# Dense products of an MLP and two gated stages by seven quarter products in place of eight

## Chip, cores and metric

One core of one Trainium2 chip runs the program. The metric is the device time of one execution in microseconds, the median of several executions.

## What is computed

Two transformer-like blocks on 1024 tokens of width 1024, float32, one after the other. Cut to what matters here:

```python
def first_block(x, ...):
    ...                                   # mixer: pooling, gated linear recurrence, w_out
    z = rms_norm(h, norm_mlp_g)
    h = h + square(relu(z @ w_up)) @ w_down          # 1024 -> 4096 -> 1024
    z = rms_norm(h, norm_ple_g)
    h = h + sigmoid(z @ w_ple_gate + b_ple_gate) * (p @ w_ple_proj)
    return rms_norm(h, norm_final_g)

def swiglu(x, w_in, w_out):
    gate, up = split(x @ w_in, 2)                    # 1024 -> 2 x 2816
    return (silu(gate) * up) @ w_out                 # 2816 -> 1024

def second_block(x, ...):
    x = x + 0.5 * rms_norm(swiglu(rms_norm(x, ffn1_pre_g), ffn1_w_in, ffn1_w_out), ffn1_post_g)
    ...                                   # mixer: dilated attention and an S5 state space model
    return x + 0.5 * rms_norm(swiglu(rms_norm(x, ffn2_pre_g), ffn2_w_in, ffn2_w_out), ffn2_post_g)
```

## The kernel before

Every dense product is made exact enough by splitting both factors into a rounded part (`wh`, `zh`, `hh`; made on ScalarE with a copy) and a remainder (`wl`, `zl`, `hl`; a subtraction) and adding three products in one PSUM bank: high x high, high x low, low x high. So each 128x128 by 128x512 block of a product is three matmuls.

Weights come in pieces of 128 x 1024. `raw` loads a piece through SP's queue into one of two buffers, `fetch` rounds it on ScalarE (L282) and takes the remainder on GpSimd (L283), and `plan`, `prefetch` and `take` keep up to `NW` = 5 pieces ready ahead of their use.

A stage begins when the stage before has finished the 1024 tokens as 8 tiles of 128. `follow` runs a chain for each tile (residual or `seam`, root mean square, scaling into `xs`), and `Z.ready(half)` turns four scaled tiles with 32 TensorE transposes (L149) and splits the result (L166, L167). `ups_first` multiplies half 0 by the first four weight pieces before it asks for half 1. After that `ups` makes two pieces' products with all 1024 tokens, an activation follows (`relu2`, L610 to L613; `swiglu`, L804 to L807, where `hl` is the remainder on VectorE), and `down` multiplies two finished factor pieces by two weight pieces, tile by tile, and adds the sum into `X` or `Y` in SBUF on VectorE (L405). Up and down alternate in a loop, so the factor stays in SBUF for a short time only. The last four factor pieces are multiplied tile by tile with the next stage's chain behind each tile; at the very end the last tile is done in halves.

Beside the MLP lies preparation for the S5 model: `s5_small` (a chain of small VectorE operations) in step 1 of the loop and one `s5_eighth` in each of the steps 3 to 10. A scheduler puts each engine's instructions into a fixed order from the program's order and its own estimate of times; `after` gives it an order and makes no wait on the chip.

SBUF buffers have tags: 24 of 4 KB a partition under `u`, 8 under `x`, 4 under `s`; two each under `raw` and `xr`; five each under `wh` and `wl`. PSUM has eight banks of 128 x 512.

## Time and profile before

| | us |
|---|---|
| median of 3 runs | 3132.41 (3132.29 to 3135.37) |
| the profiled execution, its own time | 3131.91 |
| span of that execution, first to last instruction | 3130.1 |
| busy: TensorE, VectorE, GpSimd, ScalarE | 3024.4, 1432.0, 1030.5, 899.4 |
| mean granted TensorE clock | 0.983 |
| moved by DMA | 222.94 MB |

The stages on the time axis: first mixer to about 272 us, MLP to 980, gate of the first block to 1125, first gated stage to 1840, second mixer to 2405, second gated stage to the end. A busy share says how long an engine had an instruction in hand; matmuls overlap, so the distance between their starts is read beside it.

### The profile page before, as it was taken

How to read it: one execution, taken by the hardware profiler on the slowest of the kernel's cores; microseconds unless marked ns; L12 is line 12 of the kernel's file. 1: busy time of each engine (PE TensorE's matmuls, PEld its weight loads, DVE VectorE, ACT ScalarE, POOL GpSimd, SP SyncE). 2: the span in 40 equal slices, each digit the busy share in tenths (PEclk: the TensorE clock that was granted, in tenths of full speed). 3: DMA queues.
4: the chain of work that ended last, by engine and by line, in shares of the span. 5: the costliest groups of instructions: out<-in, count | busy, mean ns of one | idle time of the engine just before them, and what ended most of it. 6: DMA issues, size and time to landing. Idle time of an engine off the chain costs nothing. (4 is left out here: it accounts for less than half of the span.)

```text
span 3130.1 us, 34489 instructions
## 1 busy us (share of the span) xinstructions
PE 3024.4 (97%) x13761; PEld 2508.9 (80%) x13761; DVE 1432.0 (46%) x2421; ACT 899.4 (29%) x1461; POOL 1030.5 (33%) x658
## 2 busy tenths in 40 slices
...
GB/s 139 61 41 75 86 78 102 90 80 107 48 48 61 68 95 54 47 48 41 54 53 49 48 128 97 160 94 74 35 54 141 54 54 48 49 53 41 54 48 95
DMA packets 71154, 222.94 MB, mean 71 GB/s; under 512 B 15988, under 2 KB 16080, under 8 KB 70992
## 3 DMA queue, kind: packets, MB, share of 16 engines
...
## 5 line engine op out<-in xcount | busy, mean ns | idle before, releaser
L283 POOL TENSOR_TENSOR wl<-raw,wh 128x1024 fp32r<-128x1024 f32 (+1 forms) x254 | 615.2, 2429 | 1751.5 <-ACT wh L282 1737.9
L383 PE MATMUL b<-z,wh 128*128 128x512 f32 x3712 | 997.5, 390 | 0.0
L383 PEld LDWEIGHTS b<-z,wh 128*128 128x128 f32 x3712 | 695.9, 188 | 147.6 <-issue 1.7
L282 ACT ACTIVATE wh<-raw 128x1024 fp32r<-128x1024 f32 (+1 forms) x254 | 267.6, 1054 | 1555.1 <-PE b L397 526.8
L383 PE MATMUL b<-z,wl 128*128 128x512 f32 x1856 | 573.4, 389 | 0.0
L805 DVE TENSOR_TENSOR sw<-sw,b 128x512 f32<-128x512 f32 x88 | 57.0, 685 | 827.6 <-PE b L383 788.5
L383 PEld LDWEIGHTS b<-z,wl 128*128 128x128 f32 x1856 | 348.5, 188 | 72.8
L397 PE MATMUL b<-wl,hh 128*128 128x512 f32 x1216 | 375.6, 389 | 0.0
L397 PE MATMUL b<-wh,hl 128*128 128x512 f32 x1216 | 375.4, 389 | 0.0
L397 PE MATMUL b<-wh,hh 128*128 128x512 f32 x1216 | 375.2, 389 | 0.0
L405 DVE TENSOR_TENSOR Y<-b,Y 128x512 f32<-128x512 f32 x320 | 204.4, 683 | 186.3 <-PE b L397 186.3
L397 PEld LDWEIGHTS b<-wh,hh 128*128 128x128 f32 x1216 | 228.2, 188 | 47.5
L397 PEld LDWEIGHTS b<-wh,hl 128*128 128x128 f32 x1216 | 228.2, 188 | 47.4
L397 PEld LDWEIGHTS b<-wl,hh 128*128 128x128 f32 x1216 | 228.2, 188 | 47.4
L405 DVE TENSOR_TENSOR X<-b,X 128x512 f32<-128x512 f32 x272 | 174.0, 683 | 118.5 <-PE b L397 118.2
L611 DVE TENSOR_TENSOR r<-r 128x512 f32<-128x512 f32 x64 | 87.6, 1393 | 116.3 <-ACT r L610 116.3
L807 DVE TENSOR_TENSOR hl<-sw,hh 128x512 fp32r<-128x512 f32 x88 | 133.2, 1548 | 9.2 <-ACT hh L806 5.2
L1235 POOL TENSOR_SCALAR P<-P,den 128x640 f32<-128x640 f32 (+5 forms) x64 | 109.2, 1729 | 13.6 <-DVE den L1234 6.9
L368 PE MATMUL b<-z,wh 128*128 128x512 f32 x256 | 99.6, 399 | 1.3 <-DVE z L167 1.3
L369 PE MATMUL b<-z,wh 128*128 128x512 f32 x256 | 99.1, 394 | 1.2 <-DVE z L167 1.2
L370 PE MATMUL b<-z,wl 128*128 128x512 f32 x256 | 99.0, 392 | 0.0
L758 POOL TENSOR_TENSOR Y<-Y,g 128x1024 f32<-128x1024 f32 x23 | 55.5, 2414 | 104.8 <-ACT junk L302 104.8
(320 smaller groups left out, 3721.2 us busy)
## 6 DMA issues: line engine op xcount, KB each, us to landing
raw<-in_f_in SPq DMA_DIRECT2D x88, 512.0 KB, 3.5
raw<-in_f_out SPq DMA_DIRECT2D x44, 512.0 KB, 3.5
raw<-in_w_up SPq DMA_DIRECT2D x32, 512.0 KB, 3.5
raw<-in_w_down SPq DMA_DIRECT2D x32, 512.0 KB, 3.8
s5l<-s SPq DMA_DIRECT2D x24, 512.0 KB, 4.9
raw<-in_w_in SPq DMA_DIRECT2D x12, 512.0 KB, 3.5
X<-in_x SPq DMA_DIRECT2D x8, 512.0 KB, 7.5
xr<-in_x SPq DMA_DIRECT2D x8, 512.0 KB, 3.5
```

The costliest lines, as they stand in the source:

```text
L282: nc.scalar.activation(h, r, AF.Copy)
L283: nc.gpsimd.tensor_tensor(l, r, h.bitcast(F32), op=ALU.subtract)
L368: nc.tensor.matmul(pp, wh[:, k, :], z(0, k, sl), start=k == 0, stop=False)
L369: nc.tensor.matmul(pp, wh[:, k, :], z(1, k, sl), start=False, stop=False)
L370: nc.tensor.matmul(pp, wl[:, k, :], z(0, k, sl), start=False, stop=k == 7)
L383: nc.tensor.matmul(pp[n], w[:, k, :], z(m, k, slice(n * H, n * H + H)), start=k == 0 and w is wh and m == 0, stop=k == nk - 1 and w is wl)
L397: yield nc.tensor.matmul(pp, h[:, ts], w[:, sl], start=f == 0 and w is wh and h is hh, stop=f == len(hs) - 1 and h is hl)
L405: nc.vector.tensor_tensor(X[t][:, sl], pp, X[t][:, sl], op=ALU.add)
L611: nc.vector.tensor_tensor(r, r, r, op=ALU.mult)
L805: nc.vector.tensor_tensor(s, s, pu, op=ALU.mult)
L807: nc.vector.tensor_tensor(hl[:, sl], s, hh.bitcast(F32)[:, sl], op=ALU.subtract)
L1235: nc.gpsimd.tensor_scalar(out=p[:, :w], in0=p[:, :w], scalar1=den[:, c : c + 1], scalar2=None, op0=ALU.mult)
```

## The change

The three places `w_up`/`w_down`, `ffn1` and `ffn2` use a form of Strassen's scheme on quarters. For the product up, two weight pieces (256 hidden units) are one factor and the normalized input is the other; each is cut into four quarters, and seven quarter products (numbered 1 to 7) of sums and differences replace eight. `lefts` makes the weight side of a pair (rounding on ScalarE, remainders of the pieces themselves on GpSimd, sums and remainders of sums on VectorE). `ZS` makes the input side once for a stage: seven operands, each rounded and with its remainder, 28 buffers that stay in SBUF. `ups_s` runs the products so that the partial sums are added in PSUM: products 1, 6, 7 and 4 go through one bank, with a copy to SBUF after 1, 6 and 7; 5 and 3 through another; 2 has its own. The order in a round is 2, 3 of the pair before, 1, 4 of the pair before, 6, 5, 7.

For the product down all up products of the stage come first. `lay_by` makes the sums and differences of the activated factor (VectorE and GpSimd) and writes seven quarters of 128 x 512 for each 256 hidden units to DRAM. `down_s` then runs the products one after the other (2, 1, 5, 3, 6, 7, 4) over all hidden units, with four banks each: for a unit of two chunks (512 hidden units) it reads the quarter back, reads the weight quarter, subtracts where the product asks for it, and rounds both on ScalarE with both remainders on VectorE, into `wh` and `wl` buffers, two of five each. The last two units of a product are multiplied tile by tile. Tiles 0 to 3 are finished in product 6 and tiles 4 to 7 in product 4.

The S5 preparation moves between the down products (`aside`): `s5_small` ahead of product 2, five eighths in the MLP and three in the first gated stage. The tags become 32 `u` and no `x`; the two `raw` buffers are also loaded in a fixed order; the first stage's input goes to DRAM (`xm`) and is read back for the residual; the last tile is no longer done in halves.

```diff
+class ZS(Z):
+    late = "u"
+    RIGHT = {1: "B11", 2: "B21", 3: "B22", 4: "T4", 5: "T1", 6: "T2", 7: "T3"}
...
+    def __call__(self, p, k):
+        hi, lo = self.op[self.RIGHT[p]][k // 2]
+        return hi[:, k % 2], lo[:, k % 2]
...
+    def split(self, name, f, eng=None):
+        m = self.m
+        hi, lo = m.u("zh", F32R, [P, 2, H]), m.u("zl", F32R, [P, 2, H])
+        m.nc.scalar.activation(hi, f, AF.Copy)
+        (eng or m.nc.vector).tensor_tensor(lo, f, hi.bitcast(F32), op=ALU.subtract)
+        self.op.setdefault(name, []).append((hi, lo))
...
+        if half == 0:
+            for name, k0 in (("B21", 4), ("B11", 0)):
+                self.f[name] = []
+                for q in range(2):
+                    f = self.turned(0, k0 + 2 * q)
+                    self.split(name, f)
+                    self.f[name].append(f)
...
+        self.settle()
...
+        for q in range(2):
+            f12.append(self.turned(1, 2 * q))
+            v.tensor_tensor(f11[q], f12[q], f11[q], op=ALU.subtract)
+            self.split("T1", f11[q])
+        for q in range(2):
+            f22.append(self.turned(1, 4 + 2 * q))
+            v.tensor_tensor(f11[q], f22[q], f11[q], op=ALU.subtract)
+            self.split("T2", f11[q])
+        for q in range(2):
+            v.tensor_tensor(f12[q], f22[q], f12[q], op=ALU.subtract)
+            self.split("T3", f12[q])
+        for q in range(2):
+            self.split("B22", f22[q], g)
+        for q in range(2):
+            v.tensor_tensor(f21[q], f21[q], f11[q], op=ALU.subtract)
+            self.split("T4", f21[q])
...
-        self.pu = pool("u", 24)
+        self.pu = pool("u", 32)
...
+        if tag == "raw":
+            if self.last_raw:
+                self.after(d, self.last_raw)
+            self.last_raw = d
...
+        q.append(None)
...
+    def lefts(self, src1, src2):
+        nc = self.nc
+        v, g = nc.vector, nc.gpsimd
+        r1, r2 = self.raw(src1), self.raw(src2)
+        w = lambda tag: self.pw.tile([P, 2, H], F32R, name=tag, tag=tag)
+        res = {}
...
+        def split(x, first, second, eng):
+            hi, lo = w("wh"), w("wl")
+            nc.scalar.activation(hi.rearrange("p a b -> p (a b)"), x, AF.Copy)
+            eng.tensor_tensor(lo.rearrange("p a b -> p (a b)"), x, hi.bitcast(F32).rearrange("p a b -> p (a b)"),
+                              op=ALU.subtract)
+            for n, p in enumerate((first, second)):
+                res[p] = tuple(x[:, n].rearrange("p (k f) -> p k f", k=4) for x in (hi, lo))
+        split(r1, 1, 2, g)
+        s1, st = self.tmp("s1"), self.u("st", tag="s")
+        a11, a12, a21, a22 = r1[:, :H], r1[:, H:], r2[:, :H], r2[:, H:]
+        v.tensor_tensor(s1, a21, a22, op=ALU.add)
+        v.tensor_tensor(st[:, :H], s1, a11, op=ALU.subtract)
+        v.tensor_tensor(st[:, H:], a11, a21, op=ALU.subtract)
+        split(st, 6, 7, v)
+        self.turn = not getattr(self, "turn", False)
+        one = w("wh" if self.turn else "wl")
+        nc.scalar.activation(one[:, 0], s1, AF.Copy)
+        v.tensor_tensor(one[:, 1], s1, one.bitcast(F32)[:, 0], op=ALU.subtract)
+        res[5] = tuple(one[:, n].rearrange("p (k f) -> p k f", k=4) for n in range(2))
+        v.tensor_tensor(a21, a12, st[:, :H], op=ALU.subtract)
+        split(r2, 3, 4, g)
+        return res
+    def ups_s(self, pairs, z, use):
+        nc = self.nc
+        left, a, c, s12, s3 = {0: self.first}, {}, {}, {}, {}
+        def product(p, n, bank, start):
+            for k in range(4):
+                zh, zl = z(p, k)
+                wh, wl = left[n][p][0][:, k, :], left[n][p][1][:, k, :]
+                for i, (w, x) in enumerate(((wh, zh), (wh, zl), (wl, zh))):
+                    self.mark = nc.tensor.matmul(bank, w, x, start=start and k == 0 and i == 0,
+                                                 stop=k == 3 and i == 2, skip_group_check=True)
+        def p3(n):
+            product(3, n, c[n], False)
+            use(n, (0, 1), c[n], s12[n][:, 1])
+        def p4(n):
+            product(4, n, a[n], False)
+            use(n, (1, 0), a[n], None)
+            for x in (left, a, c, s12, s3):
+                del x[n]
+        z.ready(0)
+        for n in range(len(pairs)):
+            if n + 1 < len(pairs):
+                left[n + 1] = self.lefts(*pairs[n + 1])
+            b = self.bank()
+            product(2, n, b, True)
+            if n:
+                p3(n - 1)
+            a[n] = self.bank()
+            product(1, n, a[n], True)
+            s12[n] = self.pr.tile([P, 2, H], F32, name="s12", tag="xr")
+            nc.scalar.activation(s12[n][:, 0], a[n], AF.Copy)
+            use(n, (0, 0), b, s12[n][:, 0])
+            if n:
+                p4(n - 1)
+            else:
+                z.ready(1)
+            c[n] = self.bank()
+            if n == 0:
+                product(5, n, c[n], True)
+            product(6, n, a[n], False)
+            nc.scalar.activation(s12[n][:, 1], a[n], AF.Copy)
+            if n:
+                product(5, n, c[n], True)
+            product(7, n, a[n], False)
+            s3[n] = self.tmp("s3")
+            nc.scalar.activation(s3[n], a[n], AF.Copy)
+            use(n, (1, 1), c[n], s3[n])
+        p3(n)
+        p4(n)
...
+    def lay_by(self, hs, p, x, y, tag):
...
+        v, g = nc.vector, nc.gpsimd
+        q, c = p // 2, p % 2
+        if c == 0:
...
+        zt, wt = (self.u(name, shape=[P, 2, H], tag=tag) for name in ("hz", "hw"))
+        v.tensor_tensor(zt[:, 0], y[:, 0], y[:, 1], op=ALU.add)
+        g.tensor_tensor(wt[:, 1], x[:, 1], y[:, 0], op=ALU.subtract)
+        v.tensor_tensor(wt[:, 0], zt[:, 0], x[:, 1], op=ALU.subtract)
+        g.tensor_tensor(zt[:, 1], x[:, 0], wt[:, 0], op=ALU.subtract)
+        for i, t in enumerate((x, zt, wt)):
+            nc.sync.dma_start(out=hs[q][i][:, c].rearrange("i p f -> p i f"), in_=t)
+        nc.sync.dma_start(out=hs[q][3][0, c], in_=y[:, 1])
...
+    LEFT = {2: (0, 0), 1: (0, 1), 5: (1, 0), 3: (1, 1), 6: (2, 0), 7: (2, 1), 4: (3, 0)}
...
+    def down_s(self, hs, w, Y, done, z=None, aside={}):
...
+        ends = [self.mark]
+        def wt(b, q):
+            if (b, q) not in W:
+                p, n = qs[q]
+                t = W[b, q] = self.u("wd", shape=[P, 2, H])
+                d = nc.sync.dma_start(out=t[:, :n], in_=w[b, p : p + n].rearrange("c p f -> p c f"))
+                self.after(d, ends[max(len(ends) - 2, 0)])
+            return W[b, q]
...
+        def right(p, q):
+            n = qs[q][1]
+            sub = lambda o, x, y: v.tensor_tensor(o[:, :n], x[:, :n], y[:, :n], op=ALU.subtract)
+            if p == 2:
+                t = wt(2, q)
+                del W[2, q]
+            elif p == 1:
+                t = wt(0, q)
+            elif p == 5:
+                t = wt(0, q)
+                sub(t, wt(1, q), t)
+            elif p == 3:
+                t = wt(3, q)
+            elif p == 6:
+                t = wt(0, q)
+                sub(t, wt(3, q), t)
+            elif p == 7:
+                t = wt(1, q)
+                sub(t, wt(3, q), t)
+            else:
+                t = wt(2, q)
+                sub(t, t, wt(0, q))
+            return t
...
+        def pair(tag, x, n):
+            hi, lo = (self.pw.tile([P, 2, H], F32R, name=tag, tag=tag) for _ in range(2))
+            nc.scalar.activation(hi[:, :n], x[:, :n], AF.Copy)
+            v.tensor_tensor(lo[:, :n], x[:, :n], hi.bitcast(F32)[:, :n], op=ALU.subtract)
+            return hi, lo
+        def unit(p, q):
+            n = qs[q][1]
+            g, i = self.LEFT[p]
+            s = self.pr.tile([P, 2, H], F32, name="sd", tag="raw")
+            d = nc.sync.dma_start(out=s[:, :n], in_=hs[q][g][i, :n].rearrange("c p f -> p c f"))
+            self.after(d, self.last_raw)
+            self.last_raw = d
+            return pair("wh", s, n), pair("wl", right(p, q), n)
+        def mm(bank, un, c, t, start, stop):
+            (sh, sl), (th, tl) = un
+            ts = slice(t * P, (t + 1) * P)
+            for k, (x, y) in enumerate(((sh, th), (sh, tl), (sl, th))):
+                self.mark = nc.tensor.matmul(bank, x[:, c, ts], y[:, c], start=start and k == 0, stop=stop and k == 2,
+                                             skip_group_check=True)
+        def product(p, banks, start, out):
+            nq = len(qs)
+            head = max(nq - 2, 0)
+            for q in range(head):
+                un = unit(p, q)
+                for c in range(qs[q][1]):
+                    for t in range(4):
+                        mm(banks[t], un, c, t, start and q == 0 and c == 0, False)
+            uns = [(q, unit(p, q)) for q in range(head, nq)]
+            for t in range(4):
+                for q, un in uns:
+                    for c in range(qs[q][1]):
+                        mm(banks[t], un, c, t, start and q == 0 and c == 0, q == nq - 1 and c == qs[q][1] - 1)
+                out(t)
+            ends.append(self.mark)
+        four = lambda: [self.bank() for _ in range(4)]
+        A, B = slice(0, H), slice(H, D)
+        copy = lambda t, sl, b: nc.scalar.activation(Y[t][:, sl], b, AF.Copy)
+        plus = lambda t, sl, b: v.tensor_tensor(Y[t][:, sl], b, Y[t][:, sl], op=ALU.add)
+        def also(p):
+            for f in aside.get(p, ()):
+                f()
+        def c11(t):
+            Y[t] = self.u("Y")
+            copy(t, A, b[t])
+        def c22(t):
+            Y[4 + t] = self.u("Y")
+            copy(4 + t, B, c[t])
+        def c12(t):
+            plus(t, B, a[t])
+            done(t)
+        def c21(t):
+            copy(4 + t, A, a[t])
+            done(4 + t)
+        also(2)
+        b = four()
+        product(2, b, True, c11)
+        also(1)
+        a = four()
+        product(1, a, True, lambda t: plus(t, A, a[t]))
+        c = four()
+        product(5, c, True, c22)
+        also(3)
+        product(3, c, False, lambda t: copy(t, B, c[t]))
+        also(6)
+        product(6, a, False, c12)
+        also(7)
+        product(7, a, False, lambda t: plus(4 + t, B, a[t]))
+        if z:
+            z.flush(3)
+            z.ready(0)
+        product(4, a, False, c21)
...
+        self.first = self.lefts(*self.up_pairs()[0])
+        self.down([y[k] for k in (2, 3, 0, 1)], ws, X, done=done)
         return z
...
+    def mlp(self, z, aside={}):
...
+        def use(n, quarter, bank, other):
+            i, j = quarter
...
+            if other is not None:
+                nc.vector.tensor_tensor(o, bank, other, op=ALU.add)
+                bank = o
+            nc.scalar.activation(o, bank, AF.Relu)
+            nc.scalar.activation(o, o, AF.Square)
+            if quarter == (1, 0):
+                self.lay_by(hs, n, xy.pop((n, 0)), xy.pop((n, 1)), "s")
...
+            r = self.raw(self.xm[t], name="xr", tag="xr", after=gate)
+            nc.vector.tensor_tensor(Y[t], Y[t], r, op=ALU.add)
+            return self.root(Y[t])
...
+        self.down_s(hs, self.a["w_down"], Y, done, z, aside)
...
+    def ffn(self, n, z, seam, aside={}):
...
+        def use(p, quarter, bank, other):
+            d, up = divmod(p, 2)
...
+            if other is not None:
+                nc.vector.tensor_tensor(o, bank, other, op=ALU.add)
+                bank = o
+            if not up:
+                nc.scalar.activation(o, bank, AF.Silu)
+                return
+            nc.vector.tensor_tensor(o, bank, G[d, j][:, at], op=ALU.mult)
+            if quarter == (1, 0):
+                self.lay_by(hs, d, X.pop((d, 0)), X.pop((d, 1)), "u")
...
-        if isinstance(z, Z):
-            self.down(hs, self.take(4), Y, done=done)
-            return z
-        self.down(hs, self.take(4), Y, done=done, last=z)
+        self.down_s(hs, self.a["f%d_out" % n], Y, done, z, aside)
+        return z
...
-        aside = {e + 3: (lambda e=e: m.s5_eighth(e)) for e in range(8)}
-        aside[1] = m.s5_small
...
+        X, z = m.mlp(z, {2: [m.s5_small], 1: [part(0), part(1)], 3: [part(2)], 6: [part(3)], 7: [part(4)]})
+        m.block2(m.ple(X, z, lambda gate, add: m.enter2(X, gate, add)), {1: [part(5)], 3: [part(6)], 6: [part(7)]})
...
```

## Rows read from the trace of the kernel before

**Rows 1.** The page, part 1: busy us, share of span, instructions.
```profile
PE 3024.4 (97%) x13761; PEld 2508.9 (80%) x13761; DVE 1432.0 (46%) x2421; ACT 899.4 (29%) x1461; POOL 1030.5 (33%) x658
```

**Rows 2.** Windows: length, busy us (instructions) by engine, PEclk, DMA share, GB/s.
```profile
272.00:980.00 708.00, 707.40 (x3223) 581.59 (x3222) 459.43 (x842) 170.43 (x254) 236.04 (x224) 1.00 0.23 76
...
2405.00:3131.00 726.00, 710.07 (x3150) 588.13 (x3148) 221.50 (x303) 140.44 (x204) 166.43 (x70) 0.99 0.17 56
```

**Rows 3.** Timeline, TensorE, full clock: start us, length us, operation.
```profile
30.55 0.39 PE L368 MATMUL b<-z,wh 128*128 128x512 f32 x1
...
31.23 0.39 PE L368 MATMUL b<-z,wh 128*128 128x512 f32 x1
```

**Rows 4.** By line: count | busy us, mean ns | idle before, its releasers.
```profile
L805 DVE TENSOR_TENSOR sw<-sw,b 128x512 f32<-128x512 f32 x88 | 57.0, 685 | 827.6 <-PE b L383 788.5 <-PE b L370 37.5 <-ACT sw L804 1.7
```

**Rows 5.** Timeline, entry of the first gated stage.
```profile
1107.15 3.66 PE L149 MATMUL b<-idn,xs 128*128 128x128 f32 x32
...
1110.57 0.48 PE L368 MATMUL b<-z,wh 128*128 128x512 f32 x1
...
1126.93 0.75 DVE L121 TENSOR_SCALAR xs<-X,r 128x1024 f32<-128x1024 f32 x1
```

**Rows 6.** By line: rounding, copy from PSUM, addition in SBUF.
```profile
L282 ACT ACTIVATE wh<-raw 128x1024 fp32r<-128x1024 f32 x250 | 265.0, 1061 | 1529.2 <-PE b L397 526.8 <-PE b L383 496.5 <-issue 426.5
...
L804 ACT ACTIVATE sw<-b 128x512 f32<-128x512 f32 x88 | 47.5, 586 | 0.5 <-PE b L370 0.5
...
L595 DVE TENSOR_TENSOR X<-X,xr 128x1024 f32<-128x1024 f32 x8 | 9.8, 1221 | 0.2
```

**Rows 7.** Timeline, entry of the MLP's up products.
```profile
268.42 2.78 PE L149 MATMUL b<-idn,xs 128*128 128x128 f32 x24
...
273.04 0.50 PE L368 MATMUL b<-z,wh 128*128 128x512 f32 x1
...
281.53 0.15 DVE L316 TENSOR_SCALAR ss<-ss 128x1 f32<-128x1 f32 x1
...
282.42 0.75 DVE L121 TENSOR_SCALAR xs<-X,r 128x1024 f32<-128x1024 f32 x1
```

**Rows 8.** Timeline, entry of the second gated stage.
```profile
2381.19 4.25 PE L149 MATMUL b<-idn,xs 128*128 128x128 f32 x24 [4.38 <-DVE xs L121]
...
2391.97 0.80 PE L368 MATMUL b<-z,wh 128*128 128x512 f32 x1 [0.18 <-DVE z L167]
...
2408.56 0.75 DVE L121 TENSOR_SCALAR xs<-Y,r 128x1024 f32<-128x1024 f32 x1
```

**Rows 9.** Windows, the same entry (columns as in rows 2).
```profile
2390.00:2395.00 5.00, 4.82 (x16) 3.84 (x16) 4.60 (x10) 4.97 (x12) 2.18 (x1) 0.56 0.98 358
```

**Rows 10.** Timeline, before the MLP: GpSimd and VectorE at one time.
```profile
265.72 4.74 POOL L283 TENSOR_TENSOR wl<-raw,wh 128x1024 fp32r<-128x1024 f32 x2 [36.04 <-ACT wh L282]
...
265.84 2.31 DVE L320 TENSOR_TENSOR r<-r,n 128x1 f32<-128x1 f32 x1
```

**Rows 11.** Windows of the MLP with the small S5 part, with eighths, without either.
```profile
313.00:353.00 40.00, 40.00 (x178) 33.08 (x177) 38.67 (x112) 11.88 (x18) 10.40 (x5) 1.00 0.26 87
400.00:700.00 300.00, 300.00 (x1389) 245.50 (x1388) 229.25 (x388) 64.95 (x97) 126.43 (x149) 1.00 0.27 89
800.00:940.00 140.00, 140.00 (x619) 115.94 (x618) 58.98 (x76) 28.31 (x40) 28.93 (x13) 1.00 0.15 51
```

**Rows 12.** Groups by line, the seam's product with the gain row.
```profile
L758 POOL TENSOR_TENSOR Y<-Y,g 128x1024 f32<-128x1024 f32 x23 | 55.5, 2414 | 104.8 <-ACT junk L302 104.8
```

**Rows 13.** Timeline, end of the kernel.
```profile
3106.46 1.28 DVE L763 SCALAR_TENSOR_TENSOR Y<-Y,r,xr 128x1024 f32<-128x1024 f32 x1
...
3114.68 0.39 PE L397 MATMUL b<-wh,hl 128*128 128x512 f32 x1
```

**Rows 14.** The page, part 6: DMA issues, count, KB each, us to landing.
```profile
raw<-in_f_out SPq DMA_DIRECT2D x44, 512.0 KB, 3.5
```

**Rows 15.** Groups by line, remainder of the gated stages' factor.
```profile
L807 DVE TENSOR_TENSOR hl<-sw,hh 128x512 fp32r<-128x512 f32 x88 | 133.2, 1548 | 9.2 <-ACT hh L806 5.2
```

302 lines of the change are left out of this document (139 added, 163 removed).

## Prediction, made before the changed kernel ran

> **What bounds the kernel now.** I read the page's busy shares first [rows 1]: TensorE is busy 97% of the span, and no other engine reaches half. A busy share hides stages, so next come the windows by stage [rows 2]: in the MLP, 272 to 980 us, and in the second gated stage, 2405 to 3131, TensorE is busy 707.4 of 708 and 710.1 of 726 us at a granted clock of 1.00 and 0.99. Is a busy TensorE also a full one? The timeline of single matmuls tells [rows 3]: three steps of a 128x512 matmul take 31.23 - 30.55 = 0.68 us, 0.2267 us each, while each is listed as 0.39 us long; they overlap, so the step is the price of one. Last, the groups by line with what ended their idle time [rows 4]: the vector operation that evicts an up product stood idle 827.6 us, of which 788.5 waited for TensorE. So the dense stages are bound by the number of matmuls, and the other engines wait.
>
> **What the change removes.** The loops give the matmuls. MLP: 32 pieces x 8 k x 3 terms x 2 halves = 1536 up, 32 x 3 x 16 = 1536 down. Each gated stage: 2112 up, 1056 down. Together 9408. Afterwards an up pair takes 7 products of 12 (84 for 96), and a down product takes 12 per chunk of 256 rows (84 for 96 as well). One eighth goes: 1176 x 0.2267 = **266.7 us**, all of it on the path, since TensorE sets the end of these stages [rows 1 to 4]. This can't fail to happen: the count stands in the loops. The 64 transposes per input stay.
>
> **What it adds.** I go by stage and ask which wait is late next.
>
> *A, entry of an up stage (three times).* Before, half 0 of the tokens is multiplied by four pieces, 96 matmuls or 21.8 us, before half 1 is asked for. Afterwards only products 2 and 1 of the first pair (24 matmuls, 5.4 us) lie ahead of `ready(1)`, and the operands T1, T2, T3 are made one after the other. From the last scaled tile to the end of product 7: 8 transposes (32 took 3.66 [rows 5]), 0.9; on ScalarE 8 evictions of about 0.59 and 6 roundings of 1.06 [rows 6], 11.1; one subtraction and one remainder on VectorE, 1.22 each [rows 6]; the last 6 matmuls, 1.4. Some 16 us. Useful work from the first transpose until then: 64 transposes, 7.3, and five products, 13.6, together 20.9. MLP: from 268.42 to 283.2 + 16 = 299.2 are 30.8, so 9.9 lost; before, matmuls began at 273.04, some 2 lost counting the pauses behind [rows 7]: +8. First gated stage: the last tile is scaled at 1127.7, 36.5 - 20.9 = 15.6 lost, none before [rows 5]: +15. Second: last tile 2409.3, 44.1 - 20.9 = 23.2 lost, 7.1 before [rows 8]: +16. Sum 39. No row shows this order; bounds 20 (half 1 overlaps half 0's chain better) to 65 (VectorE and ScalarE shared with the tile chains, and a lower clock: 0.56 after a pause of this kind [rows 9]). I take 39, which is nearest to the rows.
>
> *B, up products.* A pair is 84 x 0.2267 = 19.0 us of TensorE. Per pair ScalarE gets 3.5 roundings of 1.06, 3 copies and 8 activations of about 0.59, 10.2 us; VectorE, by 0.68 for 512 columns and 1.22 for 1024 [rows 4, 6], some 8; GpSimd two remainders of 2.37 [rows 10] and two half-size ones, 7.4. None fills 19.0. What can be late is a bank handed back. Products 1, 6, 7, 4 run through one bank with a copy in between, and product 3 goes on in the bank of product 5 once VectorE has read it: copy 0.59 plus addition 0.69 [rows 4, 6] under the one product ahead, 12 x 0.2267 = 2.72. That fits by 1.4 us. But a VectorE operation with two SBUF operands that meets a GpSimd one is held: one of 128x1 took 2.31 us while GpSimd ran [rows 10], and the addition would queue behind it. Taken: 0.3 us in each of 60 pairs, 18; bounds 0 to 60.
> The Trainium skill, "Perfetto Trace Analysis", section Optimizing Tensor Performance, asks that independent groups of matmuls rotate through different PSUM banks so that eviction overlaps the next group. This change keeps four groups in one bank on purpose; what that costs if the covering product fails to cover is a rival below.
>
> *C, starts of down products.* A down product works through units of two chunks, 24 matmuls or 5.4 us each. The rounded operands have five buffers of each kind and a unit takes two; the last two units are both held to the end. The next product's remainders can start only when the last but one is let go, 6 matmuls (1.4 us) before the end in the MLP and 3 (0.7) in the gated stages, and take 2 x 1.22 on VectorE [rows 6]. The second matmul needs both: 1.0 and 1.6 us of pause, 7 x 1.0 + 14 x 1.6 = 29, and in the MLP some 0.7 again when the last unit is readied, 5. Sum 34, bounds 10 to 50.
>
> *D, VectorE in the down products.* Before, GpSimd makes the remainders of the weights, well ahead. Afterwards VectorE makes both: 2.44 us a unit, and 3.66 in products 5, 6, 7, 4, which subtract quarters first. In a product of the MLP (192 matmuls, 43.5 us) that is 19.5 or 29.3 us. The S5 preparation lies beside it. Its price by windows: VectorE 229.25/300 with eighths against 58.98/140 without, so 33.2 - 18.3 = 14.9 us for an eighth per 43.5 us; the small part 38.67 - 16.9 = 21.8 [rows 11]. Product 2: 41.3; product 1 with two eighths and 2.7 of eviction: 52.0; product 5: 29.3; product 3: 34.4; sum 157 under 174, of which perhaps 4 shows locally. Product 6: 46.9. Product 7, with the chains of four tiles (1.22 + 0.89 + 0.75 [rows 6, 7]) and half an input (8 x 0.69 [rows 4]): 63.8. Product 4: 40.6. Sum 151.3 against 130.6: 21 late. First gated stage (132 matmuls, 29.9): 37.7 + 49.7 + 20.1 = 107.5 against 89.7, where a tile costs 5.3 because GpSimd holds it 2.41 [rows 12] beside 1.28 [rows 13]: 18 late. Second: 84 against 90, local 3. Sum 46; bounds 5 (S5 and tile work slip into slack) to 100.
>
> *E, from up to down.* The first unit needs load 3.5 [rows 14], rounding 1.06, remainders 2.44, 7.0, under the two last products, 5.4. Taken 3 each, 9; bounds 0 to 18.
>
> *At nothing.* Loads: a product reads at most 8 x (512 + 512) KB in 43.5 us, 193 GB/s; 358 GB/s has been moved at a share of 0.98 [rows 9]. If a unit's two loads went one after the other, 7.0 for 5.4, it would cost 1.6 x 95 units = 150. The write-back of factors (1.75 MB a pair in 19 us) lies beside matmuls; SP waits for it ahead of the loads of the pair after next, which has a pair's time. The end: before, the last matmul starts at 3114.68 and the span ends at 3130.1 [rows 13]; afterwards the last four tiles come faster but GpSimd's 2.41 a tile sets the pace, so the tail stays within 8 us either way.
>
> **Sum.** The profiled execution took 3131.9 us (span 3130.1), 0.5 below the median of the runs. 3131.9 - 266.7 + 39 + 18 + 34 + 46 + 9 = **3011 us**.
>
> **Rivals.**
> 1. *The gain arrives nearly whole*: the scheduler weaves S5 and tile work into VectorE's gaps, as it does now with TensorE at 300 of 300 us [rows 11]. 20 + 5 + 15 + 5 + 0 = 45 lost: 2910. Against: look-ahead falls from five pieces to two and a half units.
> 2. *Bank handovers*: the addition is held behind a GpSimd remainder in most pairs; 2.31 + 1.28 against 2.72 and the next copy late too, 1.5 us a pair: 90 for 18, 3083. With nothing covered, 3 x 0.59 + 1.28 = 3.05 a pair, 183: 3176. For: GpSimd works 7.4 of 19 us in each pair. Against: 60% of the time it doesn't. By the Trainium skill's rule above this is what would happen; no row here has such a reuse.
> 3. *VectorE becomes the bound of the down products, and the kernel is slower.* The stages have 342 operations of 1024 columns and some 278 us of other VectorE work against 724 us of TensorE. At 1.22 they make 695. The remainders of the gated stages now average 1548 ns for 512 columns [rows 15], 0.86 above a 0.69 addition [rows 4], from being held by GpSimd. With 0.86 more each: 278 + 342 x 2.08 = 989, 266 over; with A, B and E, 3131.9 - 266.7 + 66 + 266 = 3197. It turns slower from 1.89 us an operation. Against: GpSimd's remainders of weights, which do the holding now, are gone from these stages; only S5 and the seams are left.
>
> **How the numbers follow.** Forecast 0.63, rival 1 0.13, rival 2 0.12 (0.02 of it slower), rival 3 0.10, no change 0.02. The lower ends of A to E, 35 together, give 2900, and the low end stands at 2905; their upper ends, 65 + 60 + 50 + 100 with E at 9, give 3149, not all at once, and the high end, 3125, lies four fifths of the way there and takes in rival 2's usual price; below lies 0.06, above 0.12. About 0.2% is what a measurement here can tell from no change: faster 0.86, same 0.02, slower 0.12.
>
> **What would show it.** Matmul count down by 1176. In the up stages a pair every 19.0 to 19.5 us, no idle TensorE at `ups_s` beyond 0.3 a pair; pauses of 10 to 25 us at the three entries, ended by VectorE or ScalarE; pauses of 1 to 2 us at down products, ended by VectorE; longer ones in products 6 and 7 of the MLP and of the first gated stage. Wrong if TensorE waits for DMA, if pairs come every 20.5 us (rival 2), or if the 1024-column remainders average over 1.9 us (rival 3).

## The result, and the profile after

The changed kernel takes 3096.1 us (median; 3093.8 to 3098.2) against 3132.4 (3131.6 to 3135.4), a ratio of 0.9882 with a 95% interval of 0.9865 to 0.9899: 36 us faster, where 121 were forecast. The profiled execution has a span of 3092.0 us and a mean granted TensorE clock of 0.954; before they were 3130.1 and 0.983. Below, "the changed kernel" is compared at 3096.1. In the six sets of runs the kernel before came to 3130.7 to 3132.8, so sets can be compared to about 2 us.

The page, part 1, of the changed kernel; it answers [rows 1]:

```profile
PE 2818.7 (91%) x12585; PEld 2315.5 (75%) x12585; DVE 1796.1 (58%) x2707; ACT 1284.8 (42%) x1933; POOL 1009.3 (33%) x663
```

The count of matmuls fell by 13761 - 12585 = 1176, as forecast. Two more numbers can be read from this line. The same line before, less the 266.7 us, would have TensorE busy for 3024.4 - 266.7 = 2757.7 us; it is busy for 2818.7, so the matmuls that are left take **61.0 us** longer. And it stands idle for 3092.0 - 2818.7 = 273.3 us, where it was 3130.1 - 3024.4 = 105.7: **167.6 us** more. 266.7 - 61.0 - 167.6 = 38.1 is the difference of the spans.

Where the idle time lies is told by windows (length, busy us of each engine, then granted clock, DMA share, GB/s): the first mixer; up and down of the MLP; up and down of the first gated stage; the second mixer; up and down of the second gated stage. They answer [rows 2].

```profile
0.00:281.04 281.04, 257.00 (x1089) 204.37 (x1090) 170.19 (x221) 117.62 (x168) 85.69 (x66) 0.95 0.26 91
281.04:619.90 338.86, 322.13 (x1409) 264.22 (x1407) 176.78 (x207) 179.49 (x273) 127.70 (x63) 0.97 0.38 137
619.90:1006.50 386.60, 334.12 (x1479) 269.42 (x1479) 284.19 (x511) 148.78 (x174) 73.00 (x107) 0.93 0.51 177
1118.39:1564.70 446.31, 433.02 (x1913) 355.90 (x1911) 242.45 (x285) 170.65 (x240) 155.12 (x76) 0.99 0.29 101
1564.70:1836.60 271.90, 233.27 (x1017) 188.26 (x1018) 186.98 (x289) 106.76 (x142) 47.24 (x67) 0.92 0.51 171
1836.60:2361.99 525.39, 463.97 (x2314) 398.92 (x2314) 256.76 (x607) 234.68 (x478) 287.60 (x161) 0.94 0.29 94
2361.99:2827.50 465.51, 442.35 (x1935) 363.50 (x1933) 265.73 (x340) 178.01 (x256) 153.88 (x68) 0.97 0.29 103
2827.50:3070.00 242.50, 220.98 (x925) 177.83 (x924) 138.71 (x146) 91.44 (x112) 14.45 (x6) 0.96 0.46 159
```

Length less TensorE's busy time gives 24.0 us in the first mixer; 16.7, 13.3 and 23.2 in the up stages; 52.5, 38.6 and 21.5 in the down stages, 112.6 together; and 61.4 in the second mixer. The kernel before, in the same order and with up and down of a stage in one window:

```profile
0.00:268.42 268.42, 257.00 (x1090) 203.28 (x1091) 172.27 (x218) 116.25 (x168) 88.94 (x68) 0.98 0.24 84
268.42:991.50 723.08, 721.89 (x3298) 593.89 (x3297) 468.54 (x863) 178.06 (x266) 240.24 (x226) 1.00 0.23 75
1107.15:1833.40 726.25, 725.58 (x3233) 601.28 (x3231) 227.22 (x305) 156.00 (x228) 179.37 (x85) 1.00 0.18 57
1833.40:2376.19 542.79, 474.39 (x2366) 409.24 (x2367) 262.94 (x620) 240.04 (x484) 283.63 (x160) 0.93 0.29 93
2376.19:3115.10 738.91, 729.94 (x3235) 604.51 (x3233) 238.57 (x333) 153.39 (x224) 176.51 (x74) 0.99 0.18 59
```

That is 11.4 us in the first mixer, 1.2 in the whole MLP, 0.7 and 9.0 in the whole gated stages, 68.4 in the second mixer. And the changed kernel's up stages lose nothing once they run (same columns):

```profile
340.00:608.00 268.00, 268.00 (x1184) 221.83 (x1182) 125.59 (x156) 139.50 (x216) 107.83 (x55) 1.00 0.43 154
...
1175.00:1560.00 385.00, 384.31 (x1696) 317.90 (x1695) 194.07 (x245) 131.45 (x185) 130.38 (x59) 1.00 0.30 106
```

Only in the last pair of a stage does TensorE wait for ScalarE's copies (L579, L584): 2.2 us once, in the MLP, and 0.7 in each stage.

What TensorE waited for, from the list of waits (instruction <- what ended the wait: us, times, longest):

```profile
PE po L1556 <- ACT ph L1554: 37.0, 17, 7.1
PE b L671 <- ACT wl L654: 36.1, 9, 7.2
PE b L1299 <- DVE bt L1292: 28.9, 2, 14.7
PE b L155 <- DVE xs L128: 25.6, 5, 14.9
PE b L671 <- DVE wl L655: 24.7, 16, 3.2
PE b L545 <- DVE zl L211: 21.6, 11, 4.7
PE b L545 <- ACT zh L210: 14.8, 7, 5.0
PE b L474 <- ACT X L480: 14.0, 1, 14.0
```

The first row is the second mixer's, where the kernel before has 34.5 us of this wait. L671 is the down product, and wl its second operand. L545 is the up product, waiting at the entries. The other three are of kinds that the forecast did not name. L1299 are the transposes of an S5 eighth, L155 the early transposes ahead of product 4. L474 is the output product of the first mixer, a stage that the change does not touch.

What a pause costs besides itself shows in two down products of the first gated stage, 132 matmuls each and without a wait inside; the first starts after a pause of 6.92 us, the second after none. The third row is a product of the second gated stage after a pause of 2.00 us.

```profile
1571.60:1604.00 32.40, 32.36 (x132) 26.24 (x132) 13.23 (x14) 10.39 (x13) 3.27 (x3) 0.93 0.53 178
1642.90:1673.00 30.10, 30.09 (x133) 24.59 (x131) 15.40 (x18) 11.42 (x15) 2.95 (x3) 1.00 0.44 136
...
2869.00:2900.80 31.80, 31.77 (x132) 25.84 (x133) 19.13 (x20) 10.82 (x12) 0.00 (x0) 0.95 0.66 237
```

After a pause the granted clock of the stretch is 0.93 or 0.95, part of it at 1.2 of the 2.4 GHz, and the same 132 matmuls take 1.7 to 2.3 us more. In the record of the granted clock, the stretches at 1.2 GHz hold 169.6 us of TensorE's busy time, before the change 69.2. At double the clock this work would take about half (an estimate), so the lower clock makes some 50 of the 61.0 us; where the other 11 come from is not shown. There are 38 such stretches with matmuls in them, before 16, so one more costs some 2.3 us.

### The profile page after: what moved, and what is told of

It reads as the page before. It is cut to its first block, busy times and chain, and to the rows that moved or that the text cites. A ratio compares the mean times of both kernels' runs of the same rounds, so it can differ in the third digit from the quotient of the medians.

```text
span 3092.0 us, 33969 instructions
## 1 busy us (share of the span) xinstructions
PE 2818.7 (91%) x12585; PEld 2315.5 (75%) x12585; DVE 1796.1 (58%) x2707; ACT 1284.8 (42%) x1933; POOL 1009.3 (33%) x663
## 3 DMA queue, kind: packets, MB, share of 16 engines
q8 instruction: 98, 1.61, 0.2%
## 5 line engine op out<-in xcount | busy, mean ns | idle before, releaser
L671 PE MATMUL b<-wl,wh 128*128 128x512 f32 x3192 | 763.5, 401 | 61.7 <-ACT wl L654 36.1
L671 PEld LDWEIGHTS b<-wl,wh 128*128 128x128 f32 x3192 | 613.5, 193 | 206.6 <-ACT wl L654 39.5
L545 PE MATMUL b<-zh,wh 128*128 128x512 f32 x1680 | 636.7, 394 | 19.2 <-ACT zh L210 14.8
L545 PE MATMUL b<-zl,wh 128*128 128x512 f32 x1560 | 614.8, 394 | 21.6 <-DVE zl L211 21.6
L545 PE MATMUL b<-zh,wl 128*128 128x512 f32 x1680 | 628.4, 392 | 0.0
L512 POOL TENSOR_TENSOR wl<-raw,wh 128x1024 fp32r<-128x1024 f32 x120 | 294.4, 2463 | 516.7 <-ACT wh L511 459.0
L545 PEld LDWEIGHTS b<-zh,wh 128*128 128x128 f32 x1680 | 318.9, 190 | 90.4 <-ACT zh L210 17.0
L545 PEld LDWEIGHTS b<-zh,wl 128*128 128x128 f32 x1680 | 318.9, 190 | 66.2
L545 PEld LDWEIGHTS b<-zl,wh 128*128 128x128 f32 x1560 | 296.3, 190 | 88.5 <-DVE zl L211 27.4
L655 DVE TENSOR_TENSOR wh<-sd,wh 128x1024 fp32r<-128x1024 f32 x140 | 175.8, 1257 | 223.4 <-issue 109.5
L352 POOL TENSOR_TENSOR wl<-raw,wh 128x1024 fp32r<-128x1024 f32 (+1 forms) x58 | 140.8, 2434 | 373.3 <-ACT wh L351 300.8
L655 DVE TENSOR_TENSOR wl<-wd,wl 128x1024 fp32r<-128x1024 f32 x140 | 170.5, 1219 | 14.8 <-ACT wl L654 12.1
L1083 POOL TENSOR_TENSOR Y<-Y,g 128x1024 f32<-128x1024 f32 x24 | 61.6, 2575 | 276.4 <-ACT junk L376 276.4
L1537 POOL TENSOR_SCALAR P<-P,den 128x640 f32<-128x640 f32 (+5 forms) x64 | 109.4, 1727 | 13.3 <-DVE den L1536 13.0
```

The costliest lines, as they stand in the source:

```text
L352: nc.gpsimd.tensor_tensor(l, r, h.bitcast(F32), op=ALU.subtract)
L512: eng.tensor_tensor(lo.rearrange("p a b -> p (a b)"), x, hi.bitcast(F32).rearrange("p a b -> p (a b)"), op=ALU.subtract)
L545: self.mark = nc.tensor.matmul(bank, w, x, start=start and k == 0 and i == 0, stop=k == 3 and i == 2, skip_group_check=True)
L655: v.tensor_tensor(lo[:, :n], x[:, :n], hi.bitcast(F32)[:, :n], op=ALU.subtract)
L671: self.mark = nc.tensor.matmul(bank, x[:, c, ts], y[:, c], start=start and k == 0, stop=stop and k == 2, skip_group_check=True)
L1083: nc.gpsimd.tensor_tensor(Y[t], Y[t], G, op=ALU.mult)
```

## The experiments

Theory: TensorE executes in order, and so do the queues that feed it. An instruction that stands there ahead of its operand holds everything behind it. Rivals are the terms of the forecast: VectorE's load in the down products (D), held units and buffers at the product starts (C), cover at the entries (A).

### The S5 preparation

In the MLP an eighth's transposes and small matmuls stand ahead of a down product. The chain of the first two (start, length, engine, operation):

```profile
670.41 0.33 SPq L1264 DMA_DIRECT2D sxy<-sxb  x1
...
673.92 0.94 SPq L1277 DMA_DIRECT2D xy<-sxy  x1
...
682.01 0.69 DVE L1290 TENSOR_TENSOR bt<-xy,s5k 128x512 f32<-128x512 f32 x1 [2.29 <-DMA xy<-sxy]
...
685.32 1.11 PE L1299 MATMUL b<-idn,bt 128*128 128x128 f32 x4 [14.28 <-DVE bt L1292]
...
704.68 1.11 PE L1299 MATMUL b<-idn,bt 128*128 128x128 f32 x4 [14.67 <-DVE bt L1292]
```

The small part writes the factors to DRAM at 670.41; the eighth reads them back, combines them on VectorE and GpSimd, and only then can the transposes run. The second eighth has to wait for the first one's buffer. Product 1 stands behind both.

**e1**, one eighth per product, the first of them a product later:

```diff
-{2: [m.s5_small], 1: [part(0), part(1)], 3: [part(2)], 6: [part(3)], 7: [part(4)]}
+{2: [m.s5_small], 5: [part(0)], 3: [part(1)], 6: [part(2)], 7: [part(3)], 4: [part(4)]}
```

> The changed kernel with the same S5 work, but in the MLP's down products one eighth of it per product, and the first of them three products later than the small part that it reads. Theory 1 (the loss comes from instructions that wait at the head of TensorE's queue for a late operand): the waits of 14.28, 14.67 and 4.34 us at the S5 transposes of product 1 go, and with them the slow clock behind them (the stretch 670 to 715 had TensorE busy 14.5 of 45 us): 30 to 45 us less than 3096, about 3058. Theory 2 (the loss is VectorE's load in the down products): the same instructions, so no gain, 3090 to 3100.

Measured 3080.4, 15.7 less: half of what the theory said. (The first eighth stands two products behind the small part, not three as the expectation has it.) Both waits are gone, but product 1 now waits 6.19 us for its own second operand at 677.8, a wait that the eighths had covered, and each moved eighth waits up to 2.8 us again at its new place.

**e2**, only the first eighth is computed:

> The changed kernel with only the first eighth of the S5 preparation computed; the later stage reads that eighth's result in place of all eight, so seven eighths of this preparation are left out and the output is not the reference's. It prices all of that work inside the down products. Theory 1 (late operands at TensorE's queue): the first eighth, with its wait of 14.3 us, stays; the second eighth's 14.67 and its slow clock go, with the transposes and products of seven eighths: about 35 to 50 us less, most of it from one place. Theory 2 (VectorE's load): 39 us of the prediction's term for S5 at least, spread over all products, so that every product with an eighth in it gets shorter by 3 to 5 us.

Measured 3049.9, 46.2 less, some of it the left-out work on TensorE itself (140 small matmuls and transposes). The down stage of the MLP shortened by 31.5 us, that of the first gated stage by 15.3: the cost sits where the two waits were, as the theory has it, but not there alone. This run can't part waits from work; the next one can.

**e10**, every eighth in two phases, load and elementwise work a product ahead of the transposes:

```diff
-    def s5_eighth(self, e):
+    def s5_a(self, e):     # load, bt, s5c
+    def s5_b(self, e):     # transposes, small matmuls, the rest
...
-{2: [m.s5_small], 1: [part(0), part(1)], 3: [part(2)], 6: [part(3)], 7: [part(4)]}
+{2: [m.s5_small], 1: [A(0)], 5: [B(0), A(1)], 3: [B(1), A(2)], 6: [B(2), A(3)], 7: [B(3), A(4)], 4: [B(4)]}
...
-{1: [part(5)], 3: [part(6)], 6: [part(7)]}                               # first gated stage
+{2: [A(5)], 1: [B(5), A(6)], 5: [B(6), A(7)], 3: [B(7)]}
```

> The changed kernel with each eighth of the S5 preparation cut in two: its load and its elementwise part are issued one product earlier than its transposes and small matmuls, one eighth per product, in both stages. No work is left out. Theory (an aside's matmuls stand in TensorE's queue ahead of a product and wait for their operand, here made a whole product earlier): no wait at the S5 transposes is left, 3065 to 3078, less than the 3080 of the experiment that only spread the eighths, since its waits of 2.7 and 2.8 us at them go too. Rival (the S5 work slows the products through VectorE and ScalarE, wherever it lies): 3080 or more.

Measured 3062.7, **33.4 less**, with the same work on every engine; 15.7 of it came by e1's spreading alone. (The profiled execution took 3071.1, the other three 3062.2 to 3062.8.) The transposes now run between the matmuls of product 1 without a wait; what stands at its start is the second operand:

```profile
678.76 13.91 PE L671 MATMUL b<-wl,wh 128*128 128x512 f32 x52 [6.21 <-ACT wl L654]
692.51 0.38 PE L1311 MATMUL b<-idn,bt 128*128 128x128 f32 x2
692.65 5.74 PE L671 MATMUL b<-wl,wh 128*128 128x512 f32 x24
```

Some of the gain lies elsewhere. In the changed kernel the last eighth stands ahead of product 6 of the first gated stage, and its work on VectorE and GpSimd lasts until 1766, beside the chain of tiles that the early transposes wait for. With this eighth ahead of product 3 (e10) that wait falls from 14.86 to 6.19 us; without it (e2) to 6.73:

```profile
1749.10 6.17 PE L155 MATMUL b<-idn,xs 128*128 128x128 f32 x32 [6.73 <-DVE xs L128]
```

From the start of product 7 to these transposes it is 50.0 us in the changed kernel and 47.8 in e1, which left this eighth in place, but 43.1 in e10 and 42.4 in e2. So in this place S5 work beside the chain costs, as the forecast's D had it.

### VectorE's load

**e6**, the second operand's remainder by GpSimd:

```diff
-v.tensor_tensor(lo[:, :n], x[:, :n], hi.bitcast(F32)[:, :n], op=ALU.subtract)
+eng.tensor_tensor(lo[:, :n], x[:, :n], hi.bitcast(F32)[:, :n], op=ALU.subtract)   # wl: nc.gpsimd
```

> The changed kernel with the remainder of the second operand in the down products made by GpSimd instead of VectorE: 140 operations of 1.22 us, 170 us in all, leave VectorE. Theory of the prediction's step D (VectorE's load in the down products is the cost): 30 to 46 us less than 3096. Rival (order and lateness, not load, cost it): GpSimd is slower for one remainder (2.4 us against 1.22), so each late unit gets later, 5 to 40 us more than 3096.

Measured 3162.0, 65.9 more, worse than the rival's own range. By line (count | busy, mean ns | idle before): the moved remainders, and the ones that VectorE kept.

```profile
L655 POOL TENSOR_TENSOR wl<-wd,wl 128x1024 fp32r<-128x1024 f32 x140 | 393.2, 2813 | 361.6 <-PE b L671 257.9 <-ACT wl L654 87.3 <-issue 6.8
...
L655 DVE TENSOR_TENSOR wh<-sd,wh 128x1024 fp32r<-128x1024 f32 x140 | 211.8, 1516 | 282.5 <-PE b L671 225.4 <-PE b L545 27.8 <-ACT wh L654 20.9
```

Half of the remainders left VectorE, and the kernel got slower. GpSimd needs 2.81 us for one in the mean, and VectorE's own rise from 1.26 to 1.52 beside it. Their time did not leave VectorE, though: it is busy for 1801.5 us, where it was 1796.1, since what stayed takes longer. So the run shows that the move loses; what a lighter VectorE would give, it does not show.

### The starts of the down products

**e3**, one held unit instead of two (`head = nq - 1`), tests step C as it was put:

> The changed kernel, with one held unit instead of two at the end of each down product, so that one more weight unit of the next product is prepared ahead. Theory 1 (pauses at the starts of products come from the weight units that are not yet prepared): the pauses of 1 to 3 us at some 18 product starts are halved, 20 to 30 us less than 3096. Theory 2 (VectorE's load sets the pace of a whole product): a unit prepared earlier only moves the wait to a later unit, within 6 us of 3096. Against both: a held unit fewer may leave the write-back of a product less cover, then up to 10 us more.

Measured 3101.7, 5.6 more. The pause at the start of product 1 of the second gated stage grew from 2.00 to 4.64 us. **e8** gives the first operand's loads four buffers as well, in products 2, 1, 5 and 3:

```diff
-head = max(nq - 2, 0)
+head = nq - (1 if p in (2, 1, 5, 3) else 2)
-s = self.pr.tile([P, 2, H], F32, name="sd", tag="raw")
+s = self.pr.tile([P, 2, H], F32, name="sd", tag="xr" if self.flip and p in (2, 1, 5, 3) else "raw")
```

> The changed kernel with one held unit instead of two in the products 2, 1, 5 and 3 of each down stage, and with four buffers instead of two for the first operand's loads there. The experiment with one held unit alone gave no gain; there the load of the first operand waited 6.3 us in SyncE's queue for a buffer, with the second operand's loads behind it. Theory (look-ahead: held units and load buffers together limit what is ready at a product's start): the pauses of 2 to 3 us and their successors of 1.3 to 2.9 us ahead of products 1, 5 and 3 go, some 12 to 25 us less than 3096. Rival (the order on ScalarE sets it: the next unit's rounding stands behind the copy of the last bank, so buffers don't matter): pauses of 2.0 us stay, within 5 us of 3096.

Measured 3096.1: no change. Its SyncE rows ahead of that product start (4.62 us of pause) tell why:

```profile
2854.32 11.14 SPq L663 DMA_DIRECT2D sd<-hs  x3
2865.55 2.73 SPq L624 DMA_DIRECT2D wd<-in_f_out  x5
```

Three loads of the first operand hold SyncE for 11.14 us, where an issue alone takes 0.43: each waits there for a buffer. The second operand's loads are issued behind them, at the moment when the product should start. In the changed kernel four such loads hold SyncE from 2843.65 for 16.17 us, and two loads of weights follow at 2859.91. So neither of the two expectations had it: not the buffers, nor the order on ScalarE, but the order on SyncE.

**e15**, weights of products 1, 5 and 3 loaded a product ahead, one for each unit of the product before:

```diff
+NEXT = {2: 0, 1: 1, 5: 3}
 un = unit(p, q)
+if p in NEXT:
+    wt(NEXT[p], q)
```

> The changed kernel with the second operand's loads for products 1, 5 and 3 issued one product ahead, one per weight unit of the product before. Theory (the pauses at product starts come from SyncE's in-order queue: a first operand's load waits there for its buffer, and the next product's weights are issued behind it): the pauses of 2.0 us ahead of products 1 and 3 and the 3.1 in the MLP go, with their slow clock: 10 to 25 us less than 3096. Rival (held units and rounding buffers set it, as the prediction's step C had it): the pauses stay, within 5 us of 3096.

Measured 3072.0, **24.1 less**. The pauses of 3.1, 2.0, 2.0 and 2.0 us at these starts are gone; in the second gated stage TensorE runs through the boundary at 2850.0:

```profile
2835.72 15.35 PE L671 MATMUL b<-wl,wh 128*128 128x512 f32 x67
2851.77 22.97 PE L671 MATMUL b<-wl,wh 128*128 128x512 f32 x100 [0.70 <-DVE wl L655]
```

One place got worse: product 2 of the MLP takes 58.3 us instead of 48.0, since the added loads stand in the same queue ahead of its own. Most of this is hidden, for the S5 transposes behind it then wait 18.2 us where they waited 28.9.

**e14**, the first weights of a down stage allowed out once product 2 of the last up pair is done:

```diff
-ends = [self.mark]
+ends = [self.emark]    # after product 2 of the last pair
```

> The changed kernel with one ordering rule altered: the first weight loads of a down stage may be issued once product 2 of the last up pair is done, not after the last up matmul. Theory (the crossing from up to down waits for loads that are issued too late): the pauses of 3.1, 6.9 and 7.2 us at the three crossings and the slow clock behind them shrink, 12 to 22 us less than 3096. Rival (the write-back of the last pair stands ahead of these loads in SyncE's queue, or rounding is late for another reason): within 5 us of 3096.

Measured 3096.5: no change, and again SyncE's rows tell why.

```profile
1564.05 0.36 SPq L605 DMA_DIRECT2D hs<-h  x1
1566.80 0.33 SPq L307 DMA_DIRECT2D xr<-xa  x1
1567.23 2.23 SPq L625 DMA_DIRECT2D wd<-in_f_out  x4
```

The weights go out right behind a load of the residual, which the up stage holds back by its buffer. Whether the crossings can be shortened was not tried further.

### The entries and the seams

**e5** runs products 2 and 1 of the second pair ahead of the second half of the tokens, 5.4 us more cover:

> The changed kernel, but at each up stage's entry products 2 and 1 of the second pair run too before the second half of the tokens is asked for: 24 more matmuls, 5.4 us, of cover in three stages. Theory (the entries lose because too little work lies between the two halves): up to 5.4 us each and the clock behind the pauses, 10 to 20 us less than 3096. Rival (the entries lose because the chains on ScalarE and VectorE that make the second half's operands start late, whatever is ahead): the same wait comes later, within 6 us of 3096.

Measured 3108.6, 12.5 more. The wait came back, longer: in the first gated stage TensorE is busy for 66.2 us of the 82 from 1118 at a clock of 0.83, against 69.4 at 0.94. More cover in this place makes the second half later: its transposes (L202) now wait 5.5 us for a scaled tile, where they waited 0.3.

**e4** leaves the early transposes ahead of product 4 out (`z.flush(3); z.ready(0)` go):

> The changed kernel without the early start of the next stage's first transposes ahead of product 4; they come after it instead. Theory 1 (late operands at TensorE's queue): the waits of 14.86 and 4.20 us in the first gated stage and of 5.5 us in the MLP go, and the slow clock behind them (1780 to 1806: 0.72 granted): 15 to 25 us less. Rival: the transposes are then at the crossing itself, with nothing between them and the next stage's first products, and the same wait comes back there: within 6 us of 3096, or up to 10 us more.

Measured 3099.7, 3.6 more. The wait came back at the crossing, as the rival said:

```profile
1838.46 5.60 PE L155 MATMUL b<-idn,xs 128*128 128x128 f32 x32 [15.43 <-DVE xs L128]
```

**e11** puts them into product 4, ahead of its last two units:

> The changed kernel with the early transposes of the next stage moved from ahead of product 4 into it, ahead of its last two weight units: 19 us later in the gated stages, 31 us in the MLP, with 11 us of matmuls left behind them. Theory (late operand at TensorE's queue; the scaled tiles are there by then): the waits of 14.9, 5.5 and 4.2 us go without coming back at the crossing, 15 to 30 us less than 3096. Rival (the chain of tile operations on VectorE is itself late to the crossing, as leaving the early start out suggested): the wait returns behind the transposes, within 6 us of 3096.

Measured 3091.5, 4.6 less, between the two. In the MLP the 5.5 us went; in the first gated stage product 4 started 9.4 us late and paused another 6.2. There the chain itself is late. Four tiles now come at once, and their final additions in the changed kernel are 7.2 us apart:

```profile
1767.37 1.28 DVE L1090 SCALAR_TENSOR_TENSOR Y<-Y,r,xr 128x1024 f32<-128x1024 f32 x1
...
1774.69 1.28 DVE L1090 SCALAR_TENSOR_TENSOR Y<-Y,r,xr 128x1024 f32<-128x1024 f32 x1
...
1789.09 1.28 DVE L1090 SCALAR_TENSOR_TENSOR Y<-Y,r,xr 128x1024 f32<-128x1024 f32 x1
```

**e20** moves the gain's product in that chain from GpSimd to VectorE (`nc.gpsimd` to `nc.vector` at L1083):

> The changed kernel with the seams' product of a tile with its gain row made by VectorE instead of GpSimd: 24 operations of 1.22 us for 24 of 2.4 to 2.6, and VectorE no longer held beside them (remainders of 1.22 took 3.42 us there). At the first gated stage's seam four tiles now come at once, and their additions follow each other every 7.2 us (1767.4, 1774.7, 1781.9, 1789.1). Theory (this chain sets the 14.9 us wait of the early transposes and the 22 us after the last matmul): a tile every 5 us or less, 9 us less in the first gated stage, a few at the end of the kernel: 8 to 20 us less than 3096. Rival (VectorE's load, now 1.22 us a tile more, sets it): within 5 us of 3096, or slower.

Measured 3087.4, 8.7 less, but its runs spread from 3079.8 to 3096.2 and its interval (0.9837 to 0.9876) overlaps the changed kernel's. The wait that it was to shorten is 14.81 us, as before; the last addition starts at 1786.7 instead of 1789.1. Inconclusive alone, and the theory of this run does not hold for that wait.

### A stage that the change does not touch

In the first mixer of the changed kernel ScalarE's copies of the output product X (L480) stand behind two roundings (L1431) that wait for a scan on VectorE, and TensorE, whose banks are not copied out, stands still. The change's merged buffer tag is the likely reason for the new order; no run sets the tags apart, so this is not shown.

```profile
188.41 1.06 ACT L1431 ACTIVATE hi<-lth 128x1024 fp32r<-128x1024 f32 x1 [4.66 <-DVE lth L818]
193.83 1.06 ACT L1431 ACTIVATE hi<-lth 128x1024 fp32r<-128x1024 f32 x1 [4.36 <-DVE lth L818]
...
195.42 0.80 PE L474 MATMUL b<-wh,hi 128*128 128x512 f32 x1 [13.99 <-ACT X L480]
```

**e21** emits the output product ahead of the whole chain:

> The changed kernel with two lines of the first mixer in another order: its first output product is emitted ahead of the last two roundings of its input, so that ScalarE's copies of that product out of PSUM don't stand behind these roundings. The change's merged buffer tag had put them there, in a stage that the change does not touch: TensorE stood still for 13.99 us at 195.4. Theory (it is a new order on one engine, nothing that the computation needs): the pause goes, 10 to 17 us less than 3096. Rival (the roundings are what the next product waits for, and come later for it): the pause comes back some microseconds later, within 4 us of 3096.

Measured 3098.9: no gain. The pause moved to 213.2 and is 12.95 us long, since the scan chain moved back too. **e24** leaves the chain where it was and moves only the roundings:

```diff
-y[6], y[7] = self.lru_out(st)
+th = self.lru_out(st, late=True)
 X = [self.u("X") for _ in range(NT)]
 self.down([y[4], y[5]], self.take(2), X, init=True)
+y[6], y[7] = (self.hilo(t) for t in th)
```

> The changed kernel with the last two roundings and remainders of the first mixer's input emitted behind its first output product, and the scan chain that they read left where it was; the run that moved chain and roundings together only shifted the pause from 195.4 to 213.2. Theory (an order on ScalarE): the copies out of PSUM now stand between the chain's steps as before the change, TensorE works through 181 to 195, and the 14.0 us pause goes without coming back: 10 to 17 us less than 3096. Rival (the roundings are due at that time in any order): a pause of the same length some microseconds later, within 4 us of 3096.

Measured 3081.7, **14.4 less**. The copies stand between the steps of the chain, and TensorE is busy for 25.00 of the 25 us from 175 to 200, where it was 11.01:

```profile
184.41 1.07 ACT L480 ACTIVATE X<-b 128x512 f32<-128x512 f32 x2
185.37 1.06 ACT L811 ACTIVATE lth<-lth 128x1024 f32<-128x1024 f32 x1
186.32 1.58 ACT L480 ACTIVATE X<-b 128x512 f32<-128x512 f32 x3
```

So the pause came from an order on one engine, and from nothing that the data ask for.

### Do the causes add?

> The S5 preparation in two phases, the weights loaded a product ahead and the earlier loads at the crossings, all three in one kernel. If the three causes are separate pauses, their gains add: the 33 us of the two phases, and what the other two give alone, so 3025 to 3050. If they are one and the same shortage (VectorE's time, say), the sum falls short by half or more: 3055 or above.

e10, e15 and e14 together: 3060.5, which fell short; 57 us were to be had by the single runs, 35.6 came. In it product 2 of the MLP takes 58.6 us instead of e10's 47.3: e15's added loads now stand ahead of what e10 had put there.

> S5 in two phases, weights loaded a product ahead, the first mixer's copies first and the seams' gain on VectorE, all in one kernel. The first two together give some 36 us by the runs so far (without the crossing's rule, which gave nothing). If the causes are separate: 3060 less what the other two give alone, 3030 to 3045. If they share one shortage, 3055 or more.

With e20's and e21's edits and without e14's: 3053.2, in the gap between the two expectations; e21's pause is still there (12.22 us at 211.5).

> S5 in two phases, weights loaded a product ahead, the split of the first mixer's output and the seams' gain on VectorE. The same set with the other order in the first mixer gave 3053.2. If the 14.0 us pause goes here too: 3033 to 3043. If not, 3050 to 3056.

e10, e15, e20 and e24: 3031.7, a little below the first range. And the same with only the first two units loaded ahead (`if p in NEXT and q < 2`), e26:

> The same set as in the combination before, but only the first two weight units of the next product are loaded ahead, not all. With all of them ahead, the MLP's product 2 took 58.6 us instead of 47.3: the added loads stand ahead of its own in SyncE's queue. Theory (only the units at a product's start need to be early): 5 to 12 us less than that combination. Rival (the later units need it as well): the same within 4 us, or slower.

Measured **3010.2** (3002.8 to 3011.2), 21.5 less than e25 and more than was expected; the ratio to the kernel before is 0.9605 (0.9592 to 0.9618). It beats both kernels: 122 us below the kernel before, 86 below the changed one, with the same arithmetic. Product 2 of the MLP is at 47.3 us again. Its page, part 1:

```profile
PE 2792.0 (93%) x12585; PEld 2296.1 (77%) x12585; DVE 1775.1 (59%) x2731; ACT 1284.4 (43%) x1933; POOL 975.3 (32%) x639
```

This is its fastest execution (3002.8). TensorE is 64.4 us less idle (3000.9 - 2792.0 = 208.9 against 273.3), and the same matmuls take 26.7 us less: with enough of the pauses gone, the clock comes back. The single gains, 33.4 + 24.1 + 14.4 + 8.7 = 80.6, come to 85.9 here; the rule `q < 2` was not run alone. That the result is the forecast's number is chance: its losses are 103.2 us of idle time and 34.3 of slower matmuls, and not the forecast's terms.

## Why the prediction was wrong

The direction and the saving held: 1176 matmuls, 266.7 us, as said. Against them the sum set 146 us, and 228.6 came. Term by term, in idle time of TensorE:

| term | said | idle measured | from |
|---|---|---|---|
| A, entries | 39 | 42.4 | up stages 16.7 + 13.3 + 23.2, less 10.8 before |
| B, up products | 18 | about 0 once they run | 268.00 of 268, 384.31 of 385 us busy |
| C + D, down products | 80 | 95.4 | down stages 112.6, less the crossings |
| E, crossings | 9 | 17.2 | 3.1 + 6.9 + 7.2 |
| first mixer, second mixer, end | 0 | 12.6 | +12.6, -7.0, +7.0 |
| slower matmuls | in A's bounds only | 61.0 busy | page, part 1 |

**The step that failed is the price of a pause: the sum has no term for matmuls at the lower clock.** It added pauses as if each cost its own length. The text knew the lower clock, but used it only for the upper bound of A, by one row of an entry [rows 9]. Of the 82.6 us that the sum was short, 61.0 are slower matmuls, some 50 of them by the lower clock; the other 21.6 are idle time, by the rows of the table. For 167.6 us of new idle time 61.0 is 0.36 each in the mean, but it is no price per microsecond. e24 took out one pause of 14.0 us, and TensorE was busy 2.1 us less (2816.6); the profiled execution of e10 is 22.6 us less idle (3069.3 - 2818.6 = 250.7) and as long busy (2818.6); e1's is 18.3 us less idle and 11.7 longer busy (2830.4). What the rows above show is some 2 us behind a single pause, long or short. The Trainium skill, "TensorE: Matmul & The Clock Gate", section "HAM oscillation — how this bites in real kernels", says that matmuls which wait for data between groups fall back to the lower clock and pay for it on top of the wait. The trace agrees: 32.40 against 30.10 us for the same 132 matmuls.

**A** was right in its mechanism and in size as idle time (42.4 for 39; 4.3 of the 42.4 are the last pairs' waits for copies, which belong to B). **B** was too high: rival 2 did not come. The Trainium skill, "Perfetto Trace Analysis", section "Optimizing Tensor Performance", asks for different PSUM banks, so that one group's eviction overlaps the next group's matmuls. Here four groups in one bank cost nothing where a product of 2.72 us lies between them (268.00 of 268 us busy).

**C and D** came near in sum (80 and 95.4), mostly for the wrong reasons, so that nearness is chance. C blamed held units and rounding buffers; e3 and e8 gave nothing, and e15 showed the cause, SyncE's order, worth 24. D counted VectorE's microseconds for each product and priced the excess; e10 kept every operation and won 33. The two longest S5 waits cost what they did because the transposes stand in TensorE's queue ahead of a product and wait for a DMA, a GpSimd and a VectorE step in turn; the change put each eighth whole ahead of a down product. The forecast's list said "longer ones in products 6 and 7"; the longest of the MLP stood at product 1, with a chain in it that no load figure shows. One part of D held: it had the last products of the first gated stage 18 us late by S5 work and tile chains, and TensorE waits 14.9 us there behind product 7, 6.2 to 6.7 without S5 work beside the chain (e10, e2). That GpSimd's product paces these tiles did not hold: in e20 the wait is 14.8. Rival 3 is refuted by the remainders' means, 1320 and 1278 ns for 1024 columns (1257 and 1219 with the shorter ones), where it needed 1.89 us.

**Loads** were put at nothing by their mean rate. What held the second operand was the order on SyncE (e8, e15), and its loads landed in 6.4 to 8.3 us, not 3.5. The price of 150 named there counts 95 units; the loops give 140, 14 of them half as long, so it should be 1.6 x 133 = 213. The sum did not use it.

**"At nothing" left out one pause of 14.0 us** in the first mixer, a stage for which the sum had no line. e24 shows it as an order on ScalarE; that the merged buffer tags brought this order is likely and not shown. It is new against the mixer before, which lost 11.4 us in all. The end, put at "within 8 us", is 7.0 longer.

**E** was too low by 8: the pauses are 6.9 and 7.2 us in the gated stages. The two last products, which were to cover the first unit, hardly do; even when the weights may go out earlier, they do so behind a load of the residual (e14).

What stays open: the rest of the wait for the first gated stage's tiles (6.2 us in e10, 9.8 in e26), the crossings, the 11 us of slower matmuls outside the stretches at 1.2 GHz, and why e26 gained 21.5 us where 5 to 12 were expected; 10.9 of it are product 2 of the MLP (58.2 us in e25, 47.3 in e26).
